# A hybrid layer on one core: squared queries between the convolution's blocks, casts behind other ScalarE work, the last gates in ordinary banks

## The chip, the cores and the metric

The kernel runs on one core of a Trainium2 chip. A core has five engines that each take their own program in order: TensorE (PE, with its weight loads shown apart as PEld), VectorE (DVE), ScalarE (ACT), GpSimd (POOL) and SyncE (SP), which here does little else than issue DMAs. The metric is the device time of one execution in microseconds; the profile's span runs from the first to the last instruction.

## The reference

One layer of a decoder trunk on x of 1024 tokens by 1024 channels, all in float32:

```python
xn = rms_norm(x, norm_mix)
q_nsa, kv_nsa, g_nsa, conv_in, q_mem, g_merge = split(xn @ w_in)
# A: sparse attention, 8 heads of 64 in 2 groups: compressed keys, 16 chosen blocks of 64, a window of 512,
#    each with its own softmax, summed with sigmoid gates g_nsa
br_nsa = nsa_attention(...) @ w_nsa_out
# B: a * sigmoid(ag), causal depthwise convolution of 31 taps, LayerNorm over 512 channels, silu
br_conv = silu(layer_norm(conv(a * sigmoid(ag)))) @ w_conv_out
# C: cross-attention of 4 heads of 128 into 256 memory tokens, queries and keys RMS-normed
br_mem = softmax(qm @ km.T * 128**-0.5) @ vm @ w_mem_out
gm = sigmoid(g_merge)                       # three gates per channel
h = x + (gm[0] * br_nsa + gm[1] * br_conv + gm[2] * br_mem) @ w_out
out = h + (silu(rms_norm(h) @ w_gate) * (rms_norm(h) @ w_up)) @ w_down
```

## The kernel before, in words

**Products.** TensorE multiplies in fp32r, a shorter format. A float32 operand is held as two tiles, a high part and a low part, and a product is three matmuls (`mm3`): high by high, high by low, low by high. `split` makes the parts: ScalarE casts the source to the high part (L131), and VectorE, or POOL where the caller says so, subtracts it from the source (L132). Nearly every matmul has line L146, and nearly every cast L131, so the tiles' names tell what a row is: `ps` and `pf` are PSUM banks, `wsl` and `fsl` weights in two parts, `st` and `fst` their landing buffers, `slab`, `t4` and `t2` working tiles.

**Stages, in program order.** The memory queries of 128 tokens at a time (`queries(..., 0, ...)`) are projected and stored to DRAM (`qraw`). `square_queries` then loads each unit again (L354), scales it by its root mean square on POOL, turns its 32 by 32 squares on DVE and stores it with four DMAs (L367) in the order in which the memory attention reads it. The convolution follows: four blocks of 128 channels (L450), each with two column weights, four chains of 24 matmuls, a sigmoid and a product on VectorE; the 31 taps of a block are VectorE's work, spread along later projections. Then come the keys and values of A, the compression, the memory's keys and values, the memory attention, the sparse attention, the merge of the branches, `w_out` and the feed-forward part.

**Memory attention** (`mem_attention`, L645 on): eight units of 256 tokens and two heads. A unit's queries are loaded and split (POOL takes the low parts), PE makes the scores, DVE the maxima (L603), ScalarE four exponentials (L607), POOL the division (L613); DVE turns the probabilities, four DMAs store them to `pd`, one loads them again as a slab (`mem_load`). Two units later `mem_out` casts that slab (L131, `slab<-slab`), POOL subtracts its low part, and PE multiplies by the values; the output goes to `md`. Between the units stand the projections of A's queries.

**Sparse attention** works on 16 pairs of a 128-token tile and a head group; per pair there are two window units and two selected units of two heads each. For a selected unit VectorE takes the scores out of PSUM, ScalarE exponentiates (L787 for the compressed part, L801 for the rest), POOL multiplies by the gates (L726). `values` transposes the probabilities on PE (L901 for the compressed part, L915), splits them, and multiplies by the values; `heads_out` copies the result (L886).

**Merge gates as fillers.** The 3 × 8 tiles of the merge gates, each of two halves of 24 matmuls (L963 on), depend on nothing but xn. They run at a low priority and fill gaps. Each weight of 512 KB comes through one `fst` buffer, each half uses the single bank `pf` (`fbank`), is copied by ScalarE (L975) and stored to `zd` by a DMA that ScalarE issues. The first 12 tiles are free, the others are spread over the attention.

**Merge.** `unit(md[k], ...)` loads and splits the four slabs of branch C's output. Then, for the branches in the order C, A, B, each of four `w` units (two 128-channel tiles each) is multiplied with the branch's four slabs, and the product with the sigmoid of the gate from `zd` is summed. The second and third branch take their banks from `anybank`, which gives them `pf` for one product in eight.

**Order.** A scheduler with a simulated timeline fixes each engine's program from priorities and dependencies; `follow(m, i, why)` adds an edge that only sets the order: m stands behind i in the program. Buffers: 3 `wsl`, 2 `fsl`, 2 `st`, 1 `fst`, 6 `t2`, 4 `t4`, and PSUM pools of 3, 2 and 2 banks beside `pf`.

Of the kernel before, what the change touches and what calls it, by code (L numbers as in the profile page):

```python
# [8 lines left out]
F32 = mybir.dt.float32  # L9
F32R = mybir.dt.float32r  # L10
BF16 = mybir.dt.bfloat16
AF = mybir.ActivationFunctionType
# [5 lines left out]
P = 128  # L18
# [21 lines left out]
def hybrid_layer_kernel(  # L40
# [224 lines left out]

    def unit(src, shape, alloc=wslab, eng=None, load=False):
        if alloc is fslab:
            st = fstp.tile([P] + shape, F32, tag="fst", name=nm("fst"))
        else:
            st = stage.tile([P] + shape, F32, tag="st", name=nm("st"))  # L270
        ld = nc.sync.dma_start(st, src)
        w = alloc([2] + shape)
        split(w[:, 0], w[:, 1], st, eng)
        return (w, ld.ins) if load else w
# [141 lines left out]
    stat_rms(rqm)  # L416
    for t in range(NT):
        square_queries(0, t, rqm)

# [30 lines left out]
    for ct in range(4):  # L450
        wag = col_unit(w_in, C_AG + ct * P)
        wa = col_unit(w_in, C_A + ct * P)
        uc = slab([2, S], F32)
        U.append(uc)
        for half in range(2):
            pg = chan_proj(wag, half)
            sg = t2([512])
            nc.scalar.activation(sg, pg, AF.Sigmoid)
            pa = chan_proj(wa, half)
            nc.vector.tensor_tensor(uc[:, 0, half * 512:(half + 1) * 512], pa, sg, op=OP.mult)  # L460
        taps += [(ct, s) for s in range(TAPS)]
        first_tap = first_tap or len(products)


# [115 lines left out]

    msc = float(P) ** -0.5

# [9 lines left out]
    def mem_softmax(hp, tp, QM):  # L592
# [11 lines left out]
        for tt in range(2):  # L604
            for h in range(2):
                j = 2 * tt + h
                nc.scalar.activation(pm[:, tt, h, :], bs[tt][:, h, :], AF.Exp, scale=msc, bias=nb[:, j:j + 1],  # L607
                                     accum_out=den[:, j:j + 1])
        nc.vector.reciprocal(rec, den)
# [22 lines left out]
    def mem_out(hp, tp, PT):  # L632
        split(PT[:, 0], PT[:, 1], PT[:, 1].bitcast(F32), nc.gpsimd)
        o = bank([2, 256])
        for h in range(2):
            hh = 2 * hp + h
            for mb in range(2):
                ph, pl = (PT[:, hl, mb, :, h].rearrange("p a t s -> p t a s") for hl in range(2))
                mm3(o[:, h, :].rearrange("p (t a s) -> p t a s", t=2, a=4), VM[:, 0, mb, hh * P:(hh + 1) * P],
                    VM[:, 1, mb, hh * P:(hh + 1) * P], ph, pl, mb == 0, mb == 1)  # L640
        om = t2([2, 256])
        nc.vector.tensor_copy(om, o)
        nc.sync.dma_start(md[2 * hp:2 * hp + 2, :, tp * 256:(tp + 1) * 256].rearrange("h p t -> p h t"), om)
# [83 lines left out]

    QS, OB, QN, PC, WT, WP, WF, anchors, behind, tails, exps = {}, {}, {}, {}, {}, {}, {}, [], [], [], []
    wd = drp.tile([2 * NT, 20, 32, 4, P], F32, tag="wd", name="wd")
# [163 lines left out]
    def values(u, tiles):  # L893
# [4 lines left out]
        if br == 0:  # L898
# [3 lines left out]
            pt = t2([4, P], F32R)  # L902
            split(pt[:64], pt[64:], b[:64])
            m = mm(o.rearrange("p h q -> p (h q)"), vcmp[:, g, :], pt.rearrange("p h q -> p (h q)"), True, False)
# [17 lines left out]
        anchors.append((WB + nb, m.ins))  # L922

    load_q(0, 0)
    turn_q(0, 0)
# [36 lines left out]
    with low(FILL):  # L962
        for n_ in range(3 * KT):  # L963
# [3 lines left out]
            for h_ in range(2):  # L967
                ps = fbank([512])
                for k in range(KT):
# [58 lines left out]
    branches = ((2, w_mem_out), (0, w_nsa_out), (1, w_conv_out))  # L1028
    nxt, conv = [unit(md[k], [S], alloc=slab) for k in range(4)], []
    steps = layer_norm(conv)  # L1030
# [413 lines left out]
```

## Time and profile before

| | |
|---|---|
| median of three runs | 1683.01 us (1681.71 to 1685.23) |
| the profiled execution | 1683.0 us, span 1680.8 us |
| mean granted TensorE clock | 0.995 |
| PE busy | 1641.7 us, 7904 matmuls |
| PEld busy | 1369.4 us |
| DVE busy | 1062.7 us |
| ACT busy | 731.6 us |
| POOL busy | 647.0 us |

A row of a timeline begins with the start and the duration in microseconds, then engine, line, operation and tiles (out<-in). In brackets stands the idle time of the engine ahead of the row, and what ended it. A busy time counts modelled matmul ends, so two matmuls that follow each other overlap by a little.

### The profile page before, as it was taken

How to read it: one execution, taken by the hardware profiler on the slowest of the kernel's cores; microseconds unless marked ns; L12 is line 12 of the kernel's file. 1: busy time of each engine (PE TensorE's matmuls, PEld its weight loads, DVE VectorE, ACT ScalarE, POOL GpSimd, SP SyncE). 2: the span in 40 equal slices, each digit the busy share in tenths (PEclk: the TensorE clock that was granted, in tenths of full speed). 3: DMA queues.
4: the chain of work that ended last, by engine and by line, in shares of the span. 5: the costliest groups of instructions: out<-in, count | busy, mean ns of one | idle time of the engine just before them, and what ended most of it. 6: DMA issues, size and time to landing. Idle time of an engine off the chain costs nothing.

```text
span 1680.8 us, 22473 instructions
## 1 busy us (share of the span) xinstructions
PE 1641.7 (98%) x7904; PEld 1369.4 (81%) x7904; DVE 1062.7 (63%) x1800; ACT 731.6 (44%) x1345; POOL 647.0 (38%) x551
## 2 busy tenths in 40 slices
PE   7999999899999999998998999999999999999999
PEld 6878799787888888887886888888888888888887
DVE  6329889897666677766577526864554555466665
ACT  6321154443377777775456324532322223233432
POOL 0010001572168786774125401475556776400000
PEclk9999999999999999999999999999999999999999
DMA  8242245564345565555654314233334445793763
GB/s 285 74 122 53 76 163 158 176 208 146 94 129 176 171 181 141 166 167 185 218 164 151 126 51 159 75 113 105 101 105 138 146 156 185 275 401 116 229 230 124
DMA packets 247253, 262.11 MB, mean 156 GB/s; under 512 B 23956, under 2 KB 171716, under 8 KB 246118
## 3 DMA queue, kind: packets, MB, share of 16 engines
q1 hardware_dynamic: 240230, 248.10, 46.7%
q10 hardware_dynamic: 6912, 12.59, 2.0%
q8 instruction: 62, 1.02, 0.3%
q14 instruction: 49, 0.40, 0.1%
HBM read 181.99 MB, written 78.64 MB: 155 GB/s over the span
## 4 chain that ended last, share of the span: by engine, by line
PE 85%; DVE 5%; DMA 3%; ACT 3%; POOL 2%; issue 1%; SPq 0%; POOLq 0%; ACTq 0%; DVEq 0%
PE ps L146 52%; PE pf L146 17%; PE ps L1378 11%; PE ps L915 1%; PE pf L1378 1%; DVE slab L447 1%; PE ps L236 1%; DMA t<-zd 1%; POOL slab L1059 1%; DMA slab<-pd 1%; DVE slab L132 0%; DMA gn<-in_nsa_qk_norm_dram 0%; ACT t L607 0%; POOL t L613 0%; DMA st<-md 0%
## 5 line engine op out<-in xcount | busy, mean ns | idle before, releaser
L146 PE MATMUL ps<-slab,wsl 128*128 128x512 f32 (+1 forms) x1628 | 362.8, 381 | 1.9 <-ACT wsl L131 1.6
L146 PEld LDWEIGHTS ps<-slab,wsl 128*128 128x128 f32 x1628 | 295.5, 188 | 62.6 <-ACT wsl L131 2.0
L146 PE MATMUL pf<-slab,fsl 128*128 128x512 f32 x1224 | 314.1, 397 | 6.0 <-ACT fz L975 6.0
L146 PEld LDWEIGHTS pf<-slab,fsl 128*128 128x128 f32 x1224 | 225.4, 189 | 52.1 <-ACT fz L975 8.4
L146 PE MATMUL ps<-slab,fsl 128*128 128x512 f32 x696 | 164.6, 391 | 2.0 <-ACT fsl L131 1.2
L447 DVE SCALAR_TENSOR_TENSOR slab<-slab,cw 128x1019 f32<-128x1019 f32 (+16 forms) x120 | 157.5, 1317 | 1.7
L146 PE MATMUL ps<-slab,slab 128*128 128x512 f32 (+1 forms) x616 | 150.3, 379 | 6.4 <-ACT slab L131 3.1
L146 PEld LDWEIGHTS ps<-slab,fsl 128*128 128x128 f32 x696 | 130.3, 188 | 31.1 <-ACT fsl L131 1.7
L1274 DVE TENSOR_TENSOR t<-ps,t 128x512 f32<-128x512 f32 x127 | 86.9, 688 | 105.9 <-PE ps L146 104.6
L146 PE MATMUL ps<-wsl,slab 128*128 128x512 f32 (+1 forms) x690 | 151.9, 366 | 0.3 <-ACT t L343 0.3
L146 PEld LDWEIGHTS ps<-slab,slab 128*128 128x128 f32 x616 | 111.3, 190 | 29.3 <-ACT slab L131 3.5
L146 PEld LDWEIGHTS ps<-wsl,slab 128*128 128x128 f32 x690 | 117.0, 191 | 19.5 <-ACT t L343 0.6
L1378 PE MATMUL ps<-wsl 128*128 128x512 f32 x495 | 118.5, 389 | 0.0
L1378 PEld LDWEIGHTS ps<-wsl 128*128 128x128 f32 x495 | 92.9, 188 | 19.3
L132 DVE TENSOR_TENSOR wsl<-st,wsl 128x1024 fp32r<-128x1024 f32 x57 | 80.5, 1412 | 36.0 <-ACT wsl L131 35.9
L131 ACT CAST wsl<-st 128x1024 fp32r<-128x1024 f32 x58 | 61.0, 1051 | 86.2 <-PE ps L146 37.6
L146 PE MATMUL ps<-slab,qt 128*128 128x384 f32 (+6 forms) x400 | 93.1, 339 | 2.6 <-DVE sm L796 2.5
L146 PE MATMUL ps<-t,slab 128*128 128x256 f32 (+1 forms) x404 | 90.5, 324 | 0.6 <-DVE t L132 0.3
L132 POOL TENSOR_TENSOR t<-t,t 128x256 fp32r<-128x256 f32 x16 | 20.4, 1294 | 175.6 <-ACT t L131 175.6
L131 ACT CAST wsl<-t 128x1024 fp32r<-128x1024 f32 x43 | 45.3, 1054 | 90.7 <-POOL t L128 37.1
L1287 POOL TENSOR_TENSOR t<-t,t 128x512 f32<-128x512 f32 x21 | 40.0, 1906 | 112.3 <-DVE t L1274 43.6
L1059 POOL TENSOR_TENSOR slab<-slab,t 128x512 f32<-128x512 f32 x32 | 48.1, 1524 | 89.5 <-DVE t L1058 89.5
(251 smaller groups left out, 2858.0 us busy)
## 6 DMA issues: line engine op xcount, KB each, us to landing
t<-in_w_down_dram SPq DMA_DIRECT2D x70, 256.0 KB, 4.2
fst<-in_w_in_dram SPq DMA_DIRECT2D x24, 512.0 KB, 4.0
zd<-fz ACTq DMA_DIRECT2D x48, 256.0 KB, 2.9
slab<-wd SPq DMA_DIRECT2D x24, 512.0 KB, 3.9
t<-zd SPq DMA_DIRECT2D x24, 512.0 KB, 4.0
st<-in_w_gate_dram SPq DMA_DIRECT2D x22, 512.0 KB, 3.8
st<-in_w_up_dram SPq DMA_DIRECT2D x22, 512.0 KB, 4.2
ad<-t SPq DMA_DIRECT2D x44, 256.0 KB, 3.0
```

The source lines that it names most:

```text
L131: m = nc.scalar.copy(hi, src)
L132: return m, (eng or nc.vector).tensor_tensor(lo, src, hi.bitcast(F32), op=OP.subtract)
L146: m = nc.tensor.matmul(o, a, b, start=start, stop=stop)
L236: m = nc.tensor.transpose(b[:, kk, tt * P:(tt + 1) * P], js[tt][:, k * P:(k + 1) * P], ident)
L447: return nc.vector.scalar_tensor_tensor(acc[:, s:], u[:, :S - s], cw[:, ct, 30 - s:31 - s], acc[:, s:], op0=OP.mult, op1=OP.add)
L915: nc.tensor.transpose(b[:, j - j0, h, :], tiles[h][:, j * P:(j + 1) * P], ident)
L1059: nc.gpsimd.tensor_tensor(a, a, z, op=OP.add)
L1274: nc.vector.tensor_tensor(o, a_, b_, op=OP.add)
L1287: nc.gpsimd.tensor_tensor(u4, u4, c22, op=OP.mult)
L1378: nc.tensor.matmul(B[t], a_, b_, start=start and k == 0 and j == 0, stop=k == FH - 1 and j == 2, skip_group_check=True)
```

## The change

```diff
-    def unit(src, shape, alloc=wslab, eng=None, load=False):
+    def unit(src, shape, alloc=wslab, eng=None, load=False, after=None):
...
-        split(w[:, 0], w[:, 1], st, eng)
+        m, _ = split(w[:, 0], w[:, 1], st, eng)
+        if after is not None:
+            follow(m, after, "cast behind")
         return (w, ld.ins) if load else w
...
     stat_rms(rqm)
-    for t in range(NT):
-        square_queries(0, t, rqm)
...
         taps += [(ct, s) for s in range(TAPS)]
         first_tap = first_tap or len(products)
+        for t in (2 * ct, 2 * ct + 1):
+            square_queries(0, t, rqm)
...
-    msc = float(P) ** -0.5
+    msc, exps = float(P) ** -0.5, []
...
-                nc.scalar.activation(pm[:, tt, h, :], bs[tt][:, h, :], AF.Exp, scale=msc, bias=nb[:, j:j + 1],
-                                     accum_out=den[:, j:j + 1])
+                exps.append(nc.scalar.activation(pm[:, tt, h, :], bs[tt][:, h, :], AF.Exp, scale=msc,
+                                                 bias=nb[:, j:j + 1], accum_out=den[:, j:j + 1]).ins)
...
     def mem_out(hp, tp, PT):
-        split(PT[:, 0], PT[:, 1], PT[:, 1].bitcast(F32), nc.gpsimd)
+        follow(split(PT[:, 0], PT[:, 1], PT[:, 1].bitcast(F32), nc.gpsimd)[0], exps[-1],
+               "parts behind the next unit's exponentials")
...
-            split(pt[:64], pt[64:], b[:64])
+            cmps.append(split(pt[:64], pt[64:], b[:64])[0].ins)
...
-                ps = fbank([512])
+                ps = (bank if n_ > 20 and h_ else fbank)([512])
...
-    nxt, conv = [unit(md[k], [S], alloc=slab) for k in range(4)], []
+    nxt, conv = [unit(md[k], [S], alloc=slab, after=cmps[-1] if k > 1 else None) for k in range(4)], []
```

The eight calls of `square_queries` for the memory queries move from ahead of the convolution into its loop, two behind each block. The cast of a probability slab in `mem_out` gets an order edge behind the exponentials of the latest unit of which the program has been written. The casts of the third and fourth `md` slab get one behind the last compressed probability tile. The second halves of the last three gate tiles take a bank of the rotation instead of `pf`. The list of exponentials that the attention appends to is the same one now. The number of matmuls, bytes and casts stays as it was.

SP's program about the convolution's first rows, before (`t2` from `qraw` is a unit's load, `qt_m` its stores):

```order
L354 DMA t2_109_706<-qraw_142 128x512
L271 DMA fst_1299_6745<-in_w_in_dram 128x8x128
L367 DMA qt_m_143<-t2_108_698 32x4x128 x4
L354 DMA t2_111_715<-qraw_142 128x512
L367 DMA qt_m_143<-t2_110_707 32x4x128 x4
L424 DMA t2_113_726<-in_conv_w_dram 31x512
L425 DMA t2_113_726<-in_conv_b_dram 1x512
```

and now:

```order
L424 DMA t2_97_654<-in_conv_w_dram 31x512
L425 DMA t2_97_654<-in_conv_b_dram 1x512
L344 DMA qraw_142<-t2_95_644 128x512
L426 DMA t2_97_654<-in_conv_ln_g_dram 1x512
L427 DMA t2_97_654<-in_conv_ln_b_dram 1x512
L433 DMA t2_99_665<-in_cmp_pos_dram 16x2x128
L356 DMA t2_112_789<-qraw_142 128x512
L271 DMA st_133_947<-in_w_in_dram 128x8x128
L356 DMA t2_114_798<-qraw_142 128x512
L369 DMA qt_m_143<-t2_113_790 32x4x128 x4
```

The convolution's rows now stand ahead of all the squares, and the squares between the blocks' weights (`st` from `w_in`).

ScalarE's program in the memory attention, before (`slab_284` holds unit 0's probabilities, L607 are the exponentials of unit 1, `t4` from `t2` are query casts):

```order
L131 CAST slab_255_1868<-st_254_1866 128x1024
L131 CAST slab_284_2033<-slab_284_2033 128x1024
L339 COPY t2_269_1950<-ps_268_1925 128x512
L343 ACTIVATE t2_270_1951<-ps_268_1925 128x512
L339 COPY t2_282_2027<-ps_281_2002 128x512
L343 ACTIVATE t2_283_2028<-ps_281_2002 128x512
L131 CAST t4_271_1956<-t2_272_1957 128x256
L607 ACTIVATE t4_273_1964,sm_276_1967<-ps_278_1969,sm_275_1966 128x256 x2
```

and now, about the same cast (L609 here are the exponentials of unit 2, L979 evicts a gate half):

```order
L979 COPY fz_1298_6742<-pf_1297_6717 128x512
L131 CAST fsl_1306_6808<-fst_1305_6806 128x1024
L980 DMA zd_138<-fz_1298_6742 128x512
L131 CAST t4_285_2035<-t2_286_2036 128x256 x2
L979 COPY fz_1302_6775<-pf_1301_6750 128x512
L980 DMA zd_138<-fz_1302_6775 128x512
L609 ACTIVATE t4_287_2043,sm_290_2046<-ps_292_2048,sm_289_2045 128x256 x2
L609 ACTIVATE t4_287_2043,sm_290_2046<-ps_293_2056,sm_289_2045 128x256 x2
L131 CAST slab_284_2033<-slab_284_2033 128x1024
```

The cast of unit 0's probabilities has moved from ahead of the exponentials of unit 1 to behind those of unit 2.

ScalarE's program at the end of the sparse attention, before (`slab_1434` and `slab_1436` are the third and fourth md slab, `t2_1260` the last compressed tile, `wsl_1438` and `wsl_1458` the first two weights of w_mem_out):

```order
L131 CAST slab_1434_8042<-st_1433_8040 128x1024
L886 COPY t2_1256_6425<-ps_1213_6207 64x512
L131 CAST t2_1260_6438<-ps_1259_6433 64x512
L131 CAST t4_1266_6467<-ps_1265_6466 128x512
L131 CAST slab_1436_8047<-st_1435_8045 128x1024
L131 CAST t4_1268_6479<-ps_1267_6478 128x512
L131 CAST t4_1270_6492<-slab_1257_6429 128x1024
L131 CAST wsl_1438_8052<-st_1437_8050 128x1024
```

and now:

```order
L889 COPY t2_1256_6425<-ps_1213_6207 64x512
L131 CAST t2_1260_6438<-ps_1259_6433 64x512
L131 CAST slab_1434_8042<-st_1433_8040 128x1024
L131 CAST t4_1268_6479<-ps_1267_6478 128x512
L131 CAST slab_1436_8047<-st_1435_8045 128x1024
L131 CAST t4_1270_6492<-slab_1257_6429 128x1024
L131 CAST wsl_1438_8052<-st_1437_8050 128x1024
L131 CAST t4_1272_6496<-ps_1271_6495 128x512
L131 CAST t4_1269_6490<-t4_1269_6490 128x512
L131 CAST t4_1274_6508<-ps_1273_6507 128x512
L131 CAST wsl_1458_8197<-st_1457_8195 128x1024
L131 CAST fsl_1420_7967<-fst_1419_7965 128x1024
```

The compressed tile stands ahead of the third md slab now. `fsl_1420`, a weight of the last gates, is cast behind `wsl_1458`; before, its cast stood ahead of this piece, 31 rows ahead of `slab_1434`'s. On PE, the product that uses it first stands ahead of the first branch's products now:

```order
L146 MATMUL ps_1258_6432<-t4_1274_6508,slab_392_2676 128x256 x3
L918 MATMUL ps_1277_6531<-identr_107,slab_1245_6358 128x128 x4
L146 MATMUL ps_1423_7998<-slab_62_403,fsl_1420_7967 128x512
L146 MATMUL ps_1444_8067<-slab_1430_8032,wsl_1438_8052 128x512 x3
L146 MATMUL ps_1444_8067<-slab_1432_8037,wsl_1438_8052 128x512 x3
```

Before, 33 matmuls of gates stood between the last selected score and the product of the last compressed tile, and now none.

More of the change, by code (lines that the diff above doesn't have):

```diff
@@ L726, in softmax_tail @@
             nc.gpsimd.tensor_scalar(tiles[h], tiles[h], rec[:, h:h + 1], gsb[:, i, c0:c0 + 1], op0=OP.mult, op1=OP.mult)
-    QS, OB, QN, PC, WT, WP, WF, anchors, behind, tails, exps = {}, {}, {}, {}, {}, {}, {}, [], [], [], []
+    QS, OB, QN, PC, WT, WP, WF, anchors, behind, tails = {}, {}, {}, {}, {}, {}, {}, [], [], []
     wd = drp.tile([2 * NT, 20, 32, 4, P], F32, tag="wd", name="wd")
@@ L922, in values @@
         anchors.append((WB + nb, m.ins))
+    cmps = []
     load_q(0, 0)
```

## The prediction

> **What bounds the kernel now.** I read the engine totals first, then a table of stretches, then TensorE's table of waits, and last the timelines around the widest losses.
>
> ```profile
> PE 1641.7 (98%) x7904; PEld 1369.4 (81%) x7904; DVE 1062.7 (63%) x1800; ACT 731.6 (44%) x1345; POOL 647.0 (38%) x551
> 80.00:107.00 27.00, 24.98 (x110) 19.24 (x109) 6.94 (x10) 4.40 (x7) 6.42 (x8) 1.00 0.62 179
> 300.00:345.00 45.00, 40.01 (x199) 33.21 (x198) 39.60 (x48) 23.47 (x60) 31.00 (x28) 0.92 0.59 180
> 345.00:400.00 55.00, 51.43 (x250) 42.73 (x249) 48.46 (x57) 25.18 (x51) 31.21 (x25) 0.97 0.70 212
> 400.00:760.00 360.00, 355.60 (x1931) 304.13 (x1930) 241.72 (x814) 233.04 (x592) 228.88 (x245) 1.00 0.50 147
> 774.00:812.00 38.00, 32.66 (x170) 27.49 (x169) 24.02 (x26) 18.00 (x26) 14.48 (x9) 0.96 0.78 252
> 860.00:930.00 70.00, 64.50 (x274) 50.72 (x274) 49.56 (x52) 37.05 (x39) 33.45 (x22) 1.00 0.47 152
> 930.00:1400.00 470.00, 470.00 (x2107) 389.65 (x2106) 255.51 (x311) 158.16 (x236) 239.12 (x157) 1.00 0.36 117
> ```
>
> The columns of a stretch are its length, then the busy time of PE, PEld, DVE, ACT and POOL, then PE's granted clock, the DMA share and GB/s. TensorE is the bound: outside 39.1 us (1680.8 − 1641.7) it always has a matmul in hand, and from 930 us on it has no gap at all. The change leaves the multiplications as they are, so it can only win or lose idle time and clock before 930 us. I price a stretch as its idle time plus its length times the clock that was missing: 300–345 us lost 4.99 + 0.08 × 45 = 8.6 us, 345–400 lost 3.57 + 0.03 × 55 = 5.2, 774–812 lost 5.34 + 0.04 × 38 = 6.9, 860–930 lost 5.5, and the 360 us of attention between only 4.4. The edits aim at the first three and the stretch from 80 us; that sets a ceiling. The span is 1680.8 us and the profiled execution took 1683.0, so 2.2 us lie outside it; the median of the runs is 1683.01, the same.
>
> **Part 1: squared queries between the convolution's blocks.** All eight units stood ahead of the convolution's small rows on SP's queue:
>
> ```profile
> 80.83 5.60 PE L146 MATMUL pf<-slab,fsl 128*128 128x512 f32 x24
> 87.11 5.74 PE L146 MATMUL pf<-slab,fsl 128*128 128x512 f32 x24 [0.68 <-ACT fz L975]
> 93.52 5.74 PE L146 MATMUL pf<-slab,fsl 128*128 128x512 f32 x24 [0.68 <-ACT fz L975]
> 99.94 5.74 PE L146 MATMUL pf<-slab,fsl 128*128 128x512 f32 x24 [0.68 <-ACT fz L975]
> 96.99 0.29 SPq L424 DMA_DIRECT2D t<-in_conv_w_dram  x1
> 331.14 0.39 PE L146 MATMUL pf<-slab,fsl 128*128 128x512 f32 x1
> 331.37 1.48 PE L146 MATMUL ps<-slab,slab 128*128 128x256 f32 x11
> 332.68 1.11 PE L146 MATMUL ps<-slab,t 128*128 128x256 f32 x8
> ```
>
> The convolution's rows were asked for at 96.99 us, so PE filled the time with four gate halves in a row. All use the one `pf` bank, and each waits for ScalarE's eviction of the one before. A 512-column matmul starts 0.23 us after the last (331.14 to 331.37) and a 256-column one 0.12 (11 in 1.31); 72 at 0.227 are 16.3 us, while the halves begin 6.28, 6.41 and 6.42 apart: 2.8 us lost. In the new order the rows go out ahead of the squares and PE goes straight to the blocks; the four halves are spread until about 330 us, with one pair still back to back, at the price of one such step, 0.9. Part 1 gives −1.9 us. The squares' eight loads, 32 stores and eight transposes now stand between the blocks' weight loads on SP and the taps on DVE. They lie beside 22 us of matmuls per block; if that cover failed, a block would wait for its weight or for DVE's product. Bounds: −2.8 (nothing left) to +3 (each of the last three blocks waits about 1, the size of the waits shown, and the pair).
>
> **Part 2: probability casts behind the next exponentials.** Before, ScalarE takes its program in order, and the cast of a unit's turned probabilities stands ahead of the next unit's exponentials:
>
> ```profile
> 284.93 1.06 ACT L131 CAST slab<-st 128x1024 fp32r<-128x1024 f32 x1 [0.21 <-DMA st<-in_w_in_dram]
> 298.20 1.05 ACT L131 CAST slab<-slab 128x1024 fp32r<-128x1024 f32 x1 [12.22 <-DMA slab<-pd]
> 301.37 0.51 ACT L607 ACTIVATE t<-ps,sm 128x256 f32<-128x256 f32 x1
> 321.04 1.05 ACT L131 CAST slab<-slab 128x1024 fp32r<-128x1024 f32 x1 [3.52 <-DMA slab<-pd]
> 322.13 0.58 PE L146 MATMUL ps<-slab,slab 128*128 128x256 f32 x1 [3.08 <-ACT slab L131]
> 323.46 6.46 PE L146 MATMUL ps<-wsl,slab 128*128 128x512 f32 x18
> 384.12 0.60 ACT L975 COPY fz<-pf 128x512 f32<-128x512 f32 x1
> 384.77 7.37 PE L146 MATMUL pf<-slab,fsl 128*128 128x512 f32 x24 [2.72 <-ACT fz L975]
> PE pf L146 <- ACT fz L975: 7.7, 8, 2.7
> PE ps L146 <- POOL t L132: 1.6, 3, 0.6
> ```
>
> From 285.99 to 298.20 ScalarE waited 12.2 us for one load; unit 1's exponentials came at 301.37. PE itself paid directly at 322.13 (3.08, on that cast), at 384.77 (2.72, on an eviction that stood behind the exponentials), and three times about 0.6 on POOL's query parts behind the late pieces. The two long waits also cost clock: 18 matmuls after the first took 6.31 us to the next group, 0.35 each. Now each cast stands behind the exponentials of the latest unit issued, two units on. The load's 4 to 5 us then lie behind a whole unit, and the 3.08 us wait with its clock should go. The part also receives the four halves from part 1, 22 us of matmuls that PE can do while ScalarE is late. Not removed: the exponentials of unit 1 still follow the cast of unit 2's queries, whose load SP issues behind the probabilities' load, and those of unit 2 now stand behind two gate evictions. Each can still hold the softmax for a few us. Of the 13.8 us of the two stretches I keep 5: the three 0.6 waits, an eviction of 2.7 as at 384.77, and 0.5 of clock. Part 2: −9. Bounds: 0 (all waits move) to −13.8 (all of it goes).
>
> **Part 3: md casts behind compressed tiles, and gates in two banks.** T0 = 774.03 is the last selected score.
>
> ```profile
> 774.03 0.33 PE L146 MATMUL ps<-klast,qt 128*128 128x128 f32 x2
> 776.88 0.60 PE L915 MATMUL ps<-identr,slab 128*128 128x128 f32 x4
> 777.24 3.46 PE L146 MATMUL pf<-slab,fsl 128*128 128x512 f32 x14
> 779.43 3.34 POOL L132 TENSOR_TENSOR slab<-slab,t 128x1024 fp32r<-128x1024 f32 x1
> 782.82 0.51 PE L146 MATMUL ps<-slab,slab 128*128 128x512 f32 x1 [1.00 <-POOL slab L132]
> 789.15 1.04 ACT L131 CAST slab<-st 128x1024 fp32r<-128x1024 f32 x1 [6.65 <-DMA st<-md]
> 790.82 1.06 ACT L131 CAST t<-ps 64x512 fp32r<-64x512 f32 x2
> 792.81 0.79 PE L146 MATMUL ps<-t,vcmp 128*128 128x512 f32 x1 [4.00 <-DVE t L132]
> 791.48 0.38 SPq L271 DMA_DIRECT2D st<-in_w_mem_out_dram  x1
> 802.20 0.38 SPq L271 DMA_DIRECT2D st<-in_w_mem_out_dram  x1
> 806.84 1.05 ACT L131 CAST wsl<-st 128x1024 fp32r<-128x1024 f32 x1 [5.21 <-DMA st<-in_w_mem_out_dram]
> ```
>
> ScalarE stood 6.65 us at the third md slab, the compressed cast stood behind it, and PE waited 4.00 us for its low part. The reordering removes exactly that. But the new program also moves work away from under this place. Before, 33 gate matmuls lie between T0 and the wait at 792.81, and they hid most of POOL's 3.34 us subtraction, which ended at T0 + 8.7. Now there are none. Ahead of the products that need POOL's result stand 11 256-column and some ten small matmuls, about 2 us, so PE waits 6.5. The last group's copy, cast and subtraction (0.58, 0.53 and about 0.7 us in a row, PE with four transposes) add 1.5. It is then T0 + 14; 24 gate matmuls, 24 of 256 columns and 16 transposes (0.09 each, from 776.88 to 777.24) are 5.4 + 2.9 + 1.4 = 9.7, to T0 + 24. There PE's program has one product of the last gates' weight `fsl_1420`, ahead of everything of the first branch. Its cast stood 45 rows ahead of that of the second w_mem_out weight on ScalarE; now it stands right behind it. The third md slab comes at T0 + 15 as before, the first weight's load follows (6.2 us from issue to cast at 791.48), and the second's about 2 us later with 4.6 (802.20 to 806.84): cast at T0 + 25 to 27, `fsl_1420` a microsecond on. PE waits another 3. In all 11, and 1 for clock: 12 against 6.9, **+5 us**. Bounds: −2 (POOL's subtraction comes as much earlier as PE does) to +13 (the second weight is as late as before, below).
>
> The Trainium skill, TensorE: Matmul & The Clock Gate, Part 1, puts the halving of the clock at an idle window of about 3.4 us. By that the waits of 3.08 and 2.72 us need not have cost any clock, and part 2 could win only its idle time, 8.6 − 3.3 = 5 us instead of 9; the rows, with 0.35 us per matmul behind the shorter wait, say otherwise, and the sum goes by them; by the rule it would come near R1's time.
>
> Behind it, the two banks show:
>
> ```profile
> 919.47 3.01 PE L146 MATMUL pf<-slab,wsl 128*128 128x512 f32 x12 [1.67 <-ACT fz L975]
> 924.11 2.14 PE L146 MATMUL ps<-slab,wsl 128*128 128x512 f32 x8 [1.62 <-ACT wsl L131]
> ```
>
> The last gate half sat in the `pf` bank from 800 to 919 us and kept out three products of the later branches, and their weights and gate loads queued up. With the last halves in ordinary banks, `pf` is free much earlier. Of the 5.5 us I take −4 (1.67 + 1.62 and what led to them). Bounds: 0, if the late weights of T0 + 27 carry through, to −5.5. In the middle of attention, waits of 4.4 us in 360 leave no more than ±2; I take 0.
>
> **Sum.** −1.9 − 9 + 5 − 4 = −9.9. Span 1680.8 − 9.9 = 1670.9, with the 2.2 outside **1673 us**.
>
> **Rivals.**
> *The memory waits only move (R1).* Behind the cast come query casts and gate evictions in the same in-order program. For it: at 384.77 PE waited for an eviction, not for a cast. Against it: the longest wait, 3.08, is on the cast itself. Then part 2 gives 4 instead of 9: 1678 us.
> *The last gates' weight holds the end of attention (R2, slower).* One mechanism: PE's program puts a product of `fsl_1420` ahead of all products of the first branch, and ScalarE casts it behind the second w_mem_out weight. If that weight arrives as before, at 806.84 = T0 + 32.8, PE stands still from T0 + 24 to T0 + 35, 18 in all with the earlier 8, 20 with clock: +13 instead of +5. The late gates delay their stores and loads too, so that the 4 from the two banks are lost, and if part 2 wins 5 the sum is −1.9 − 5 + 13 + 0 = +6: 1689. It decides once the wait at that product is above some 11 us. For it: the order of the rows. Against it: the second weight's buffer comes free at the fourth md cast now, while before another load stood ahead of it.
> *Everything fits (R3).* The end of attention costs what it did (0), the memory part wins 12, the banks 5.5, part 1 1.9: −19.4, 1664.
> *The order isn't obeyed.* The new program shows all edges on ScalarE's rows, so this gets no share.
>
> **How the numbers follow.** Forecast 0.47 (1673, own range 1668 to 1678), R1 0.20, R2 0.17, R3 0.16. About 0.2%, 3.4 us, is what a measurement tells from no change, so faster means below 1679.6. The forecast puts 0.45 there, R1 half, R3 all: 0.71. Within: 0.02 + 0.10 = 0.12. Slower: 0.17. For 8 in 10 the range takes in R1, most of R3 and the lower part of R2: 1662 to 1685.
>
> **What would show it.** Part 1: no four gate halves in a row before the first block, convolution products about 22 us earlier, no new waits on weight casts in the blocks. Part 2: the 3.08 us wait on the probabilities' cast and the 12.2 us hole on ScalarE gone, clock near 1.00 through the memory attention. Part 3: the 4.00 us wait on the compressed low part gone, waits on POOL's subtraction and on `fsl` in its place, and none on `fz` at 919. Wrong would be a memory stage that still loses above 9 us, or an end of attention that loses above 18 (R2) or under 8 (R3).

## The result, and the profile after

The changed kernel takes 1698.06 us (median of 4, 1696.34 to 1699.48) against 1683.88 us for the kernel before in the same runs: a ratio of 1.0085, 95% interval 1.0068 to 1.0102. That is 14 us slower, where 10 us faster was forecast, and outside the range. The profiled execution took 1696.9 us with a span of 1695.2.

The engine totals and the table of stretches of the changed kernel (columns as in the prediction):

```profile
PE 1650.6 (97%) x7904; PEld 1373.2 (81%) x7904; DVE 1064.8 (63%) x1800; ACT 729.8 (43%) x1343; POOL 642.6 (38%) x551
80.00:107.00 27.00, 27.00 (x120) 22.34 (x119) 13.75 (x14) 5.07 (x6) 2.79 (x2) 1.00 0.31 88
300.00:345.00 45.00, 40.00 (x190) 33.31 (x188) 26.47 (x34) 18.02 (x44) 17.57 (x20) 0.96 0.52 158
345.00:400.00 55.00, 53.46 (x272) 44.78 (x271) 47.05 (x52) 19.98 (x38) 28.82 (x21) 1.00 0.58 175
400.00:760.00 360.00, 352.02 (x1893) 296.54 (x1892) 243.51 (x825) 235.38 (x599) 226.22 (x242) 1.00 0.51 148
774.00:812.00 38.00, 32.00 (x148) 26.21 (x149) 16.03 (x17) 17.19 (x22) 15.30 (x7) 0.87 0.61 207
812.00:860.00 48.00, 40.44 (x175) 32.74 (x173) 20.15 (x25) 16.28 (x20) 0.00 (x0) 0.94 0.54 181
860.00:930.00 70.00, 67.19 (x279) 53.47 (x278) 54.52 (x51) 41.51 (x40) 25.65 (x16) 0.97 0.53 171
```

The gaps from 80 to 107 us are gone and the memory part is better, but the sparse attention, its end and the first branch of the merge are worse. From 812 to 860 us PE had no gap before; now it stands still for 7.6 us. That stretch before:

```profile
812.00:860.00 48.00, 48.00 (x212) 39.04 (x211) 25.73 (x34) 26.03 (x26) 2.39 (x1) 1.00 0.60 200
```

Stretches of time hold different work in two kernels, so I also compare at the same matmul. **Lag** is a matmul's start less the median spacings (from the trace of before) of all matmuls ahead of it. Those spacings add up to 1608.6 us in every kernel here, so the difference of two lags is lost time alone. The sixteen products with the compressed values mark the sixteen pairs of the attention.

| lag gained in | before | after | squares alone | mem alone | md alone | banks alone |
|---|---|---|---|---|---|---|
| 0 to 107 us | 17.1 | 14.2 | 15.4 | 17.2 | 17.5 | 17.3 |
| 107 to 260 us | 1.1 | 1.9 | 1.9 | 1.7 | 1.6 | 1.7 |
| to the first pair (memory part) | 17.4 | 13.1 | 15.9 | 15.8 | 15.1 | 15.1 |
| first to 15th pair | 15.5 | 22.5 | 10.9 | 24.9 | 16.3 | 18.3 |
| last pair | 6.8 | 13.2 | 4.0 | 6.8 | 4.5 | 12.7 |
| from there (merge) | 10.1 | 17.6 | 9.8 | 13.4 | 6.1 | 20.0 |
| sum | 68.1 | 82.5 | 57.9 | 79.7 | 61.1 | 85.0 |

A profiled execution can lie up to 5 us from the median of its kernel (that of parts 1 and 3 below is 4.8 us above it, that of `mem_next_unit` 4.7 below), so single differences of 1 us say nothing. The program gives a second measure, the **gate halves** (24 matmuls each, 48 in all) that PE has behind it at a point. They are its **cover**: work that it can do while others are late. Before, 13.0 stand ahead of the memory attention's end (its last score product), 21.8 ahead of the first pair and 46.8 ahead of the last; after, 14.0, 21.0 and 44.0.

Where the time came from in the changed kernel, by PE's waits and the timelines of PE, ScalarE and SP's queue (`identr` rows are transposes):

```profile
PE ps L146 <- ACT fsl L131: 7.7, 2, 7.6
PE ps L918 <- DVE t L132: 5.8, 5, 3.6
779.01 1.12 PE L918 MATMUL ps<-identr,slab 128*128 128x128 f32 x4 [3.63 <-DVE t L132]
781.21 0.63 PE L146 MATMUL ps<-t,slab 128*128 128x512 f32 x1
781.64 0.63 PE L146 MATMUL ps<-slab,slab 128*128 128x512 f32 x1
797.84 0.50 PE L146 MATMUL ps<-slab,fsl 128*128 128x512 f32 x1 [0.16 <-ACT fsl L131]
845.36 4.47 PE L146 MATMUL pf<-slab,fsl 128*128 128x512 f32 x19
845.79 1.05 ACT L131 CAST slab<-st 128x1024 fp32r<-128x1024 f32 x1 [6.88 <-PE pf L146]
857.88 1.04 ACT L131 CAST fsl<-st 128x1024 fp32r<-128x1024 f32 x1 [2.44 <-DMA st<-in_w_mem_out_dram]
858.98 9.14 PE L146 MATMUL ps<-slab,fsl 128*128 128x512 f32 x28 [7.56 <-ACT fsl L131]
853.70 0.38 SPq L271 DMA_DIRECT2D st<-in_w_mem_out_dram  x1
```

Three things are to be seen. At 779 PE waits between transposes, with no gate matmul in that piece, for a low part that stands on VectorE behind those of the first two md slabs (774.92 to 778.35), and a 512-column matmul behind it takes 0.43 us (781.21 to 781.64) instead of 0.23. At 797.84 the last gates' weight, which the slower rival made decisive, costs 0.16 us. And at 845 ScalarE's cast of the first `od` slab (branch A's output) was let go by a `pf` matmul: in the program the last gate tile's first half now comes behind its second half, and the four `od` slabs lie at the addresses of the four xn slabs that this first half reads (before, none of the four lay there). The `od` casts hold both `st` buffers, the last w_mem_out weight is loaded at 853.70 and cast at 857.88, and PE waits 7.56 us for it.

### The profile page after: what moved, and what is told of

It is laid out like the page before. It is cut to its first block, busy times and chain, and to the rows that moved or that the text cites. A ratio compares the mean times of both kernels' runs of the same rounds, so it can differ in the third digit from the quotient of the medians.

```text
span 1695.2 us, 22465 instructions
## 1 busy us (share of the span) xinstructions
PE 1650.6 (97%) x7904; PEld 1373.2 (81%) x7904; DVE 1064.8 (63%) x1800; ACT 729.8 (43%) x1343; POOL 642.6 (38%) x551
## 4 chain that ended last, share of the span: by engine, by line
PE 53%; DVE 3%; DMA 2%; POOL 2%; ACT 1%; issue 1%; SPq 0%; ACTq 0%; DVEq 0%; POOLq 0%
PE ps L146 34%; PE ps L1382 11%; PE pf L146 6%; PE pf L1382 1%; PE ps L918 1%; DMA st<-in_w_nsa_out_dram 1%; POOL slab L132 0%; DVE slab L132 0%; PE ps L236 0%; DMA t<-zd 0%; DMA st<-in_w_mem_out_dram 0%; DMA wd<-wsl 0%; POOL slab L729 0%; DVE t L1062 0%; POOL slab L1063 0%
## 5 line engine op out<-in xcount | busy, mean ns | idle before, releaser
L146 PE MATMUL pf<-slab,fsl 128*128 128x512 f32 x1152 | 293.1, 395 | 2.0 <-ACT fz L979 1.8
L146 PEld LDWEIGHTS pf<-slab,fsl 128*128 128x128 f32 x1152 | 211.0, 188 | 43.9 <-ACT fz L979 3.4
L146 PE MATMUL ps<-slab,fsl 128*128 128x512 f32 x768 | 184.7, 395 | 10.5 <-ACT fsl L131 7.7
L146 PEld LDWEIGHTS ps<-slab,fsl 128*128 128x128 f32 x768 | 145.5, 190 | 43.5 <-ACT fsl L131 8.4
L447 DVE SCALAR_TENSOR_TENSOR slab<-slab,cw 128x1019 f32<-128x1019 f32 (+16 forms) x120 | 163.5, 1367 | 1.8
L132 DVE TENSOR_TENSOR t<-ps,t 128x512 fp32r<-128x512 f32 (+2 forms) x96 | 60.9, 639 | 30.6 <-ACT t L131 29.7
```

What stands on the lines that cost most here:

```text
L132: return m, (eng or nc.vector).tensor_tensor(lo, src, hi.bitcast(F32), op=OP.subtract)
L146: m = nc.tensor.matmul(o, a, b, start=start, stop=stop)
L447: return nc.vector.scalar_tensor_tensor(acc[:, s:], u[:, :S - s], cw[:, ct, 30 - s:31 - s], acc[:, s:], op0=OP.mult, op1=OP.add)
```

## The experiments

### The parts one at a time

The four kernels undo or keep parts of the change as a whole: `squares_mem_md` is the change without

```diff
-                ps = (bank if n_ > 20 and h_ else fbank)([512])
+                ps = fbank([512])
```

and the others are the kernel before with one part.

squares_mem_md: 

> The change without the two banks (parts 1 to 3 only; every gate half in pf again). Theory B, the banks: taking the second halves of the last three gate tiles out of pf puts them into the attention's own rotation, so that one comes 24 matmuls later than before the last score, and the very last first half comes after its second half and keeps its xn slabs, which the merge's od slabs take over. Then everything lost from 740 to 860 us is the banks' doing, and this kernel gains 2.8 us in the convolution and 5 in the memory part and about 3 at the compressed tile: 1672 us, 1668 to 1677, no wait above 3 us at 774 to 860. Theory M, the moved work: the memory part's earlier progress and the squares take the fillers and the buffers from the end of the attention; then this kernel keeps the loss there and takes 1690 us or more.

banks_alone: 

> Before with part 4 alone (last three second halves in the rotation's banks). Theory B: 17 to 22 us slower than before, 1700 to 1705, with a wait of 5 to 8 us on an fsl weight near 860 and PE's clock under 0.95 about the last score. Theory M: within 4 us of before, or faster by what the pf bank no longer blocks (1679 to 1684).

mem_alone: 

> Before with part 2 alone (probability casts behind the next unit's exponentials). Theory B: the memory part wins 4 to 6 us and nothing else moves, 1677 to 1680. Theory M: the win is given back in the attention, whose lag grew by 5 us from 400 to 740 in the change: 1683 to 1690.

squares_alone: 

> Before with part 1 alone (squares between the convolution's blocks). Theory B: the three waits for the pf bank go, 2 to 3 us faster, 1680 to 1681. Theory M: the win is given back between 107 and 300 us, where VectorE is busy 138 of 153 us in the change against 124 before: 1683 to 1686.

| kernel | median us | ratio to before, interval |
|---|---|---|
| squares, mem, md (parts 1 to 3) | 1679.51 | 0.9975, 0.9963 to 0.9988 |
| banks alone (part 4) | 1699.00 | 1.0090, 1.0075 to 1.0105 |
| mem alone (part 2) | 1695.86 | 1.0070, 1.0055 to 1.0085 |
| squares alone (part 1) | 1673.50 | 0.9940, 0.9925 to 0.9955 |

The banks cost 15 us alone (1 us less than theory B's range) and 18.6 on top of the others. That is theory B for them. But parts 1 to 3 gain 5 us and not 12, and the memory order alone loses 12: theory M has the direction and the place there, though the time lies 6 us above its range. Part 1 alone gains 10.7 us, of which 1.7 stand in its own stretch. Neither theory had that.

### The banks, taken apart

`banks_21_22` is before with the condition `n_ in (21, 22) and h_`; `squares_md` is before with parts 1 and 3; `squares_md_lasthalf` adds `n_ == 23 and h_` to it.

banks_21_22: 

> Before with the second halves of tiles 21 and 22 alone in the rotation's banks, the last tile wholly in pf, in its order. 44.0 gate halves stand ahead of the last compressed tile as with all three moved, against 46.8 before; the last first half ends at 777 us of work instead of 739. Theory C1 (two losses): the missing cover costs the 8 to 9 us at the last score as with all three, and the late release of the xn slabs still holds the od slabs: 1694 to 1700, wait on fsl 4 us or more near 855. Theory C2 (only the swapped last tile costs the wait on fsl): 1690 to 1693, without that wait.

squares_md: 

> Parts 1 and 3 (squares between the blocks, md casts behind compressed tiles), no memory order, no second bank. Theory N: the squares alone had already taken the wait at the last compressed tile away (its lag from the last pair was 4.0 us with part 1 alone and 4.0 with parts 1 to 3, against 6.8), so the md order adds nothing: within 2 us of squares alone, 1672 to 1675. Theory S: the md order takes its own 3 us: 1669 to 1671.

squares_md_lasthalf: 

> The same with one gate half more: only the very last second half goes to a bank of the rotation, the other 47 stay in pf. In the program the last first half now comes ahead of it, and no gate half leaves the stretch before the last score. Theory B1 (which halves move decides): pf comes free some 100 us earlier for the merge and nothing is lost at the last score: 2 to 5 us faster than parts 1 and 3, 1668 to 1671. Theory B2 (any gate half in the rotation's banks disturbs the attention's end): 8 us slower or more.

`banks_21_22` took 1689.53 us (1.0031, 1.0017 to 1.0045). Its last pair loses 12.5 us, as with all three (12.7): both have 44.0 gate halves ahead of the last pair instead of 46.8. From there it loses 8.9 instead of 20.0, and the wait on `fsl` near 855 is 2.6 instead of 7.5. So the change of order in the last tile makes most of the loss in the merge, and the loss at the last pair comes with tiles 21 and 22, where the gate matmuls are missing. The rest of the wait stays: in this program too the four `od` slabs take xn slabs that the last gate tile reads, and that tile ends 40 us of work later than its first half did before. C1 and C2 were each half right.

`squares_md` took 1672.35 us (0.9935, 0.9912 to 0.9958), the same as squares alone, and its last pair loses 4.0 as there: theory N. The second-half version took 1675.06 (0.9948, 0.9930 to 0.9965): its early `pf` bank was worth nothing measurable, and neither B1 nor B2 holds. Its merge still loses 12.6 us; the 13.6 of parts 1 and 3 are from the longest of that kernel's four runs.

### The memory order and the gate halves

Part 2 moves halves: 18.0 stand ahead of the memory attention's end with part 2 alone, 13.0 before. The stretch from 300 to 400 us, the `pf` rows alone, before and with part 2 alone (the busy columns are PE, PEld, DVE, ACT):

```profile
300.00:400.00 100.00, 31.83 (x124) 23.75 (x122) 0.00 (x0) 3.58 (x6) 0.95 0.65 198
```
```profile
300.00:400.00 100.00, 48.23 (x202) 36.98 (x201) 0.00 (x0) 5.31 (x9) 0.97 0.56 172
```

78 more gate matmuls (18 us) run there, and the lag of the memory part falls by 1.6 us. Then all 24 free halves are spent at the first pair, and one stands in each of the next pairs where one to two stood. From the first to the seventh pair PE loses 12.9 us instead of 3.6. Two kernels test whether this is cause or company: ten free tiles instead of twelve, and an edge that holds the free tiles from the eighth on behind the memory attention.

```diff
     pt3 = mem_attention(ws)
+    mem_end = products[-1][0]
...
+                    if 7 <= n_ < N_EARLY and not k:
+                        tc.add_manual_dep(first.ins, mem_end.name, ORDER, reason="behind the memory")
```

mem_alone_ten_free: 

> Part 2 alone with 10 free gate tiles instead of 12 (the last 14 spread over the attention instead of 12). With part 2 all 24 free halves are spent before the first pair's compressed tile, 24.0 against 21.8 before, and each pair up to the fifth has one half left to cover its waits, where before had one to two. Here each has 1.0 to 1.8 from the third on. Theory F (cover): the 13 us that PE loses from the first to the seventh pair in part 2 alone shrink to 8 or less, and the time falls by 4 to 8 us to 1688 to 1692. Theory O (the memory order's own engine order or buffers cause it): the same 13 us, 1694 or more.

mem_cover_held: 

> Part 2 alone, with the free gate tiles from the eighth on held behind the end of the memory attention (an order edge only). Gate halves ahead of its end: 14.0, against 18.0 with part 2 alone and 13.0 before; from there to the seventh pair 16.0 against 12.6 and 17.6. Theory F (part 2 spends the attention's cover early): the 12.9 us that PE loses from the first to the seventh pair in part 2 alone fall to 3 to 6, near the 3.6 of before; the memory part loses more than the 10 us of part 2 alone since it has four halves less; the time falls from 1696 to 1683 to 1689. Theory O (order or buffers of part 2 itself): the loss from the first to the seventh pair stays above 9, 1694 or more.

all_but_banks_held (parts 1 to 3 with the same edge, from the sixth tile on): 

> Parts 1 to 3 with the free gate tiles from the sixth on held behind the end of the memory attention: 10.0 halves ahead of its end, as 9.0 with parts 1 and 3, against 14.0 with parts 1 to 3. Theory F: the pairs get back what they have with parts 1 and 3 (4 to 6 us less lost from the first to the tenth pair than the 13.6 of parts 1 to 3), and the memory part keeps some of part 2's gain: 1668 to 1674, no slower than parts 1 and 3 (1672). Theory O: no better than parts 1 to 3, 1678 to 1682.

| kernel | median us | halves at memory's end, first pair | memory part | first to 7th pair |
|---|---|---|---|---|
| before | 1683.88 | 13.0, 21.8 | 17.4 | 3.6 |
| mem alone | 1695.86 | 18.0, 24.0 | 15.8 | 12.9 |
| mem alone, ten free | 1698.38 | 18.2, 20.0 | 34.6 | 12.0 |
| mem, cover held | 1711.55 | 14.0, 21.0 | 40.6 | 7.1 |
| parts 1 to 3 | 1679.51 | 14.0, 21.0 | 14.2 | 6.1 |
| parts 1 to 3, held | 1696.47 | 10.0, 17.0 | 38.8 | 5.6 |

All three are slower than I said, and they fail ahead of the first pair. PE's waits from 300 to 480 us, with their stretch, before and with the cover held:

```profile
PE pf L146 <- ACT fz L975: 3.5, 3, 2.7
PE ps L146 <- ACT slab L131: 3.1, 1, 3.1
300.00:480.00 180.00, 170.50 (x834) 141.69 (x833) 140.11 (x258) 78.03 (x210) 79.42 (x77) 0.97 0.49 150
```
```profile
PE ps L146 <- ACT slab L131: 10.4, 7, 2.9
PE ps L146 <- ACT t L131: 5.9, 2, 4.5
PE ps L146 <- POOL slab L132: 3.3, 2, 2.6
300.00:480.00 180.00, 155.96 (x721) 127.97 (x720) 127.57 (x196) 60.38 (x152) 58.44 (x58) 0.92 0.43 132
```

With about as many halves ahead of its end as before, part 2 loses 23 us more in the memory part, and PE waits seven times on the very cast that was moved, where it waited once. That looks like the price of the order. But the halves do not stand in the same places. From the sixth unit's last score to the last product of the memory attention, and from there to the first pair:

| kernel | us lost to the last product | halves there | us lost on to the first pair | halves there |
|---|---|---|---|---|
| before | 6.4 | 3.4 | 1.7 | 6.4 |
| mem alone | 2.2 | 4.3 | 4.6 | 5.4 |
| mem alone, ten free | 5.6 | 4.5 | 18.6 | 1.2 |
| mem, cover held | 30.3 | 0.0 | 1.9 | 7.0 |
| parts 1 and 3 | 7.1 | 3.4 | 1.7 | 6.4 |
| parts 1 to 3, held | 24.6 | 0.2 | 3.2 | 6.8 |

Part 2 takes its halves earlier, so those that the edge allows are spent by then, and the last units run with none. With ten free tiles the hole lies behind the memory attention, in the projections of A's keys; I had priced only the pairs behind it. Each loss stands where the halves are missing. What the later cast costs by itself isn't separated from this: no run has the old order with the same hole, nor the order of the change with the old places. Part 2 looked 4 us better in the change with five more halves spent in that part, 27 us of cover that the attention then lacks: the first 15 pairs lose 18.8 us in parts 1 to 3 and 11.5 in parts 1 and 3. In the attention the cover theory holds as far as it goes: held, the pairs up to the seventh lose 7.1 instead of 12.9, not the 3 to 6 I expected, 4.9 of it in the third pair alone; and in parts 1 to 3 held, the pairs up to the tenth lose 8.0 instead of 13.3.

### One unit earlier

In the change the cast of unit u − 2 stands behind the exponentials of unit u. `mem_next_unit` (part 2 alone) and `squares_md_next_unit` (parts 1 and 3 with it) put it behind those of unit u − 1:

```diff
-        follow(split(PT[:, 0], PT[:, 1], PT[:, 1].bitcast(F32), nc.gpsimd)[0], exps[-1],
+        follow(split(PT[:, 0], PT[:, 1], PT[:, 1].bitcast(F32), nc.gpsimd)[0], exps[-5],
```

mem_next_unit: 

> Part 2 alone with the edge one unit earlier: the cast stands behind the exponentials of the unit before the latest, not of the latest. Gate halves ahead of the memory attention's end 13.5, as before (13.0; part 2 alone 18.0). Theory L (loop): in part 2 the cast of unit u-2 waits for the exponentials of unit u, which wait for scores that PE has only just made, while PE's next matmuls wait for that cast; one unit earlier that loop is open, so the memory part loses 8 to 16 us from 300 us to the first pair instead of 17.4 before, with few waits of PE on the slab cast, and the time is 1677 to 1684, 12 us or more below part 2 alone. Theory A (any delay of the cast hurts the same chain): 1690 or more.

squares_md_next_unit: 

> Parts 1 and 3 with part 2 one unit earlier (the cast behind the exponentials of the unit before the latest). 9.5 halves ahead of the memory's end, as 9.0 with parts 1 and 3. Theory L: the memory part wins 2 to 6 us on parts 1 and 3 and the attention keeps its cover: 1666 to 1671. Theory A: slower than parts 1 and 3 by 5 or more, 1677 and up.

They took 1692.93 us (1.0063, 1.0042 to 1.0084) and 1683.03 us (0.9997, 0.9987 to 1.0007). The first is 3 us better than part 2 alone, the second 10.7 slower than parts 1 and 3, and 3.5 slower than parts 1 to 3. The halves ahead of the memory's end are within 0.5 of those without part 2, the waits on the slab cast are short, as theory L said, and the memory part loses 19.7 and 18.1 us, where before lost 17.4 and parts 1 and 3 lost 16.1. Another wait is there instead. In `squares_md_next_unit`, waits of PE from 300 to 480 us and ScalarE's timeline:

```profile
PE pf L146 <- ACT fz L979: 5.3, 1, 5.3
PE ps L146 <- ACT slab L131: 1.8, 1, 1.8
356.53 0.23 ACT L349 ACTIVATE rqn<-rqn 128x32 f32<-128x32 f32 x1 [6.00 <-DVE rqn L346]
360.34 0.60 ACT L979 COPY fz<-pf 128x512 f32<-128x512 f32 x1
```

ScalarE stood 6.00 us at a root of A's queries, and exponentials and a gate's eviction behind it, so that PE waited 5.3 for its bank; the attention loses 5.4 us more too (16.9 against 11.5), of it 5.7 in the fifth pair. Theory L falls as the whole cause, since the loop is open and the time is lost all the same. That a later cast always hurts is not shown either; what is shown is that both later places of it lost, alone and with parts 1 and 3. Why the fifth pair loses 5.7 us in the one stays open.

### Md alone, and free tiles

md_alone (before with part 3): 

> Part 3 alone (md casts behind the last compressed tile). Gate halves ahead of every pair are those of before. Theory S (the edit does what it says): the wait of 4.0 us on the compressed tile goes, the last pair loses 4 instead of 6.8, and nothing else moves: 1680 to 1682. Theory N: the wait is replaced by one on POOL's low parts or on the next tile, within 1.5 us of before.

squares_md_fourteen_free (`N_EARLY = 14` in parts 1 and 3): 

> Parts 1 and 3 with 14 free gate tiles instead of 12. The free halves last until the eleventh pair (38.8 ahead of it against 37.2), with three halves per pair from the eighth to the eleventh, and 1.5 per pair behind it against 1.9. Theory F: the pairs up to the eleventh lose as little as now (0.4 to 1.2 each) and the last four a little more: within 3 us of parts 1 and 3, 1671 to 1675. Theory O gives no difference either; a loss above 4 us in the last four pairs would say that their cover is already short.

fourteen_free (`N_EARLY = 14` in before): 

> Before with 14 free gate tiles instead of 12, nothing else. Gate halves ahead of the memory's end and the first three pairs as before (13.0, 21.8, 23.0, 24.0); between the third pair and the tenth 13.6 instead of 11.6, behind it 10.9 till the last instead of 11.2. Theory F (squares alone won 4.6 us in the attention because four free halves were left for it): the tenth pair's 3.7 us fall under 1.5 as in squares alone (0.6, with 15.0 halves from the third to the tenth), and the pairs up to it lose 3 us or more less: 1678 to 1681. Theory O: the tenth pair keeps 3 us or more, within 2 us of before.

Md alone took 1676.21 us (0.9950, 0.9934 to 0.9966), 8 us faster, more than either theory. The last pair loses 4.5 instead of 6.8, as theory S had it, and the merge 6.1 instead of 10.1, which I hadn't seen. With part 1 the first is already gone (4.0), and the second does not come (13.6 in the longest run; by the medians parts 1 and 3 are 1.2 us faster than part 1 alone). The two fourteen-free kernels took 1675.23 (0.9941, 0.9923 to 0.9959) and 1687.69 (1.0019, 1.0008 to 1.0031). In the second the tenth pair's 3.7 us fell to 2.2, and the pairs from the first to the tenth lose 8.3 instead of 9.6; the later ones then lose 19.7 instead of 12.7. More cover early is less cover late. It is not the whole of what part 1 does: there the four halves come from the convolution, so nothing behind lacks them, and in the tenth pair 0.6 us are left. Neither theory is met: the 3 us of F did not come, and the tenth pair did not keep the 3 us of O.

### The merge, and the fastest version

The merge lost 6 to 20 us over the kernels so far. In md alone the last gate half was through at 791 us of work (and with ten free tiles at 790, where the merge lost 6.4), in before, squares alone and parts 1 and 3 it sat in `pf` until 852 to 854. That is no rule: in parts 1 to 3 held and in the two kernels with fourteen free tiles it was through at 790 too, and their merges lost 10.6, 13.1 and 11.3. `squares_md_gates_first` holds the second branch back for it; the bank stays `pf`:

```diff
+                        if n_ == 1 and d_ == 0 and not k:
+                            follow(m, gate_end, "behind the last gates")
```

`next_unit_gates_first` has this and the cast one unit earlier; `gates_first_fourteen_free` has this and `N_EARLY = 14`.

squares_md_gates_first: 

> Parts 1 and 3, with the first product of the second branch ordered behind the last gate half on PE, which stays in pf. The last half then ends at 795 us of work instead of 854. Theory P: the half that sits in pf until about 909 us costs the merge its waits at 888 to 917 (6.5 us in parts 1 and 3), and the md order alone escaped them since its last half ends at 791: 4 to 7 us faster than parts 1 and 3, 1666 to 1669. Theory Q: the merge's waits are on weights and gate loads whatever pf does (with the last half in another bank the time didn't move): within 2 us of 1672.

next_unit_gates_first: 

> The two last edits together on parts 1 and 3. If theories L and P both hold: 1661 to 1666, below every other kernel here. If one holds: 1666 to 1671. If neither: 1675 and up.

gates_first_fourteen_free: 

> Parts 1 and 3 with the last gate half ahead of the second branch, and 14 free gate tiles. The last pair lost 2.4 us with 14 free tiles and 4.0 with 12, the pairs before it 1 us more: within 2 us of the version with 12 (1665.5) either way. If the last pair's saving holds and nothing else moves: 1663 to 1665.

The first took 1665.50 us, 0.9899 (0.9882 to 0.9915) of before, 7 us less than parts 1 and 3 and the fastest of all. PE's waits from 812 to 930 us in parts 1 and 3, and with the edge:

```profile
PE ps L146 <- ACT fsl L131: 2.6, 2, 2.4
PE pf L146 <- DVE t L1061: 2.4, 1, 2.4
PE pf L146 <- ACT fz L978: 1.2, 1, 1.2
860.00:930.00 70.00, 63.76 (x263) 50.56 (x262) 48.27 (x48) 39.00 (x43) 31.55 (x22) 0.95 0.45 152
```
```profile
PE ps L146 <- DVE slab L132: 1.3, 1, 1.3
860.00:930.00 70.00, 68.72 (x301) 56.20 (x301) 50.24 (x57) 40.84 (x45) 36.71 (x25) 1.00 0.44 153
```

The merge's lag fell from 13.6 to 4.5. The medians differ by 6.9 us, less than the lags, since the trace of parts 1 and 3 is of its longest run. The size is theory P's. The second took 1676.17 us (0.9956, 0.9943 to 0.9969), 6.9 us less than without the edge: the gain comes there too (12.4 to 6.8), and the cast's order costs 10.7 us again, for which my expected times left no room. The third took 1673.49 (0.9933, 0.9916 to 0.9949), 8 us more than with twelve free tiles, where I expected 2 at most, and 1.7 less than without the edge. With fourteen free tiles the last half is through at 790 us of work with or without it, so the edge had little to move; its merge loses 11.7 us, with one wait of 3.65 at 845 that the profile puts down to VectorE's subtraction in the LayerNorm (L1004).

So the edge is worth 7 us where the half was late. That the held bank is the reason, as theory P has it, is not shown: with the half early (fourteen free tiles) or the last half in another bank the merge still loses 11 to 13 us. What else a good merge needs stays open.

## Why the prediction was wrong

By its own steps, in lag of the profiled executions, sum +14.5:

- **Part 1, −1.9.** Right: −2.9 up to 107 us, +0.8 up to 260; no four halves in a row, no waits on the blocks' weights. What I didn't see is that the four halves, once kept out of the convolution, are worth more in the attention. Alone they go with 4.6 us less in the pairs (17.8 halves ahead of the first pair instead of 21.8). The 2.8 us less in the last pair have another reason, since 46.8 halves stand ahead of it as before: with part 1 alone ScalarE casts the last compressed tile (779.24) ahead of the third and fourth md slab (780.56, 782.13), which is what part 3 was to bring about.
- **Part 2, −9.** This term failed. In the change the memory part won 4.3 us. I wrote that it "also receives the four halves" and booked them as a gain. It took them and one more (13.0 halves from 107 us to its last score instead of 8.0), so the pairs were left with what they had before, and lost 7.3 more than in parts 1 and 3. The step that failed is this one: cover was counted where it came in, and not where it would be missing. R1, the waits only move, is right in part: from 80 to 400 us PE waits 3.5 us on slab casts (two waits) and 1.5 on another cast, where one wait of 3.1 on a slab cast stood. (In the sum for waits that cost no clock, the idle time that I kept is 1.8 + 2.7 = 4.5 and not 3.3, so it gives 4 and not 5.)
- **Part 3, +5 at the end of attention.** From 774 to 812 us the loss was 6.0 + 0.13 × 38 = 10.9 us against my 12, which is near by luck. I had 11 of idle time and 1 of clock; it was 6.0 and 4.9. PE's long wait there was on VectorE (3.63), and POOL's subtraction, on which I had 6.5, added 0.49. The reason that I gave, no gate matmuls between the last score and POOL's subtraction, was right, but I booked it under the wrong part. The md order doesn't take them away: the last pair loses 4.0 in parts 1 to 3 and 4.5 in md alone, against 6.8 before, and 12.7 with the banks alone. The wait at `fsl_1420`, 3 us in my sum and 11 in R2, was 0.16.
- **The two banks, −4.** The term with the wrong sign, and the largest miss: +18.6 us on top of parts 1 to 3. By lag 9.2 of it stand in the last pair and 3.4 in the 15th, where the halves are missing, and 4.7 in the merge (the lags of the change against those of parts 1 to 3). I counted the bank that comes free, and neither the cover that leaves the end of the attention nor the order of the two halves, which stands in the new program. A half in another bank may come ahead of the one in `pf`, and the xn slabs of the late half are the buffers of what follows. That costs the 7.56 us at 859. The edge that only brings the last half forward gained 7 us, so the −4 was there to be had, but not through the banks.
- **The middle of the attention, 0.** I left it out, since its waits were only 4.4 us in 360. It was +7.0: 2.9 in the 15th pair, where the halves that the banks took begin to be missing, and 4.1 ahead of it. These 4.1 are not the banks': up to the tenth pair parts 1 to 3 lose 13.3 too, against 9.6 before and 7.1 in parts 1 and 3, so they come with part 2. But the pairs have as many halves as before, so the count of halves does not explain them; that stays open.

The rival on the slower side got the sign, with 0.17, and the wrong place: 1689 for a weight that came in time.

## What to carry to other kernels

Free work that fills gaps is a budget. Before pricing a reordering, count in the new program how much of it stands ahead of each later place, and price the places that lose it; a stretch that gets faster may only have spent it early. Where one of two pieces in a row gets a buffer of its own, look for the order that they come in then, and for who takes over what the late one still holds. An edge that puts a cast later has to be checked against the consumer that follows it, with the filling work held constant in every place and not only in its sum.

## What the runs showed of the hardware that I had not expected

The clock can drop behind several short waits, and stay up behind one that is longer. With the cover held, PE's longest wait from 300 to 480 us was 4.5 us and the slab waits were at most 2.9, yet the granted clock was 0.92 there, against 0.97 before: 0.08 × 180 = 14 us. In that trace the clock is 0.50 from 332.84 to 336.25 us, behind waits of 0.82 and 1.45 us, and from 401.11 to 404.52, behind 0.76, 1.53 and 0.56; behind single waits of 2.62 (to 351.03) and 2.59 (to 361.56) it stays at 1.00. The Trainium skill, TensorE: Matmul & The Clock Gate, Part 1, gives an idle window of about 3.4 us for the clock to halve. The rows here show drops without an idle stretch of that length.
